# Up projection of a gated MLP: ten of 22 pairs of weight tiles from seven block products each, x normalised before the product, gated tiles split at the end

## The chip, the cores and the metric

One core of a Trainium2 chip runs the whole program. The time is the device time of one execution in microseconds (us). The engines are TensorE (PE, with its weight loads as PEld), VectorE (DVE), ScalarE (ACT), GpSimd (POOL) and SyncE (SP), whose queue starts the loads of weights. Each engine runs its own instructions in the order of the program; one that waits holds up all behind it on that engine. The program has 1 batch, 512 tokens, a model width of 1024 and fp32 data.

## The reference, cut to what matters

The layer mixes tokens in three ways, attends to a memory of 256 tokens, and ends with a gated MLP, which the change touches:

```python
x = x + memory_cross_attention(rmsnorm(x, norm_xq), rmsnorm(mem, norm_mem), ...)
x = x + conv_ffn(rmsnorm(x, norm_ffn), w_up, ffn_conv, ffn_conv_b, w_down)

def rmsnorm(x, g):                       # y = x * rsqrt(mean(x*x) + EPS), then y * g
def conv_ffn(h, w_up, conv_w, conv_b, w_down):
    u = causal_dwconv(h @ w_up, conv_w) + conv_b      # 3 taps along the tokens
    a, b = jnp.split(u, 2, axis=-1)                   # 2816 channels each
    return (jax.nn.silu(a) * b) @ w_down
```

## The kernel before, in words

Channels lie on the 128 partitions and the 512 tokens on the free axis. The model width is 8 tiles of channels, the hidden width 22 tiles for `a` and 22 for `b`. Products are made from split operands: a value is rounded to the matmul's type (`hi`, a copy on ACT) and the rest kept beside it (`lo`, a subtraction on DVE), and each product is the sum of hi by hi, hi by lo and lo by hi (`mm3`, L181-189).

The up projection (L947-959) goes over 22 pairs. Pair m makes tiles m and m+22. Each tile takes one unit of weights, 128 partitions by 1024 (8 blocks of 128 columns, one per tile of the model width): `load_unit` loads 512 KB through SP's queue into one of three buffers, `split_unit` makes hi (L164, ACT) and lo (L165, DVE) with two buffers each, and `mm3` issues 24 matmuls of 512 columns into a PSUM bank (16 by hi, L185 and L186, then 8 by lo, L188). The inputs `xf` are x times the gain, split, not yet normalised. The factor 1/rms of a token, `r_f`, comes from a column sum of squares and is multiplied in on DVE as each tile leaves PSUM (L951). Then the convolution: bias and last tap on ACT (L953), the two other taps on DVE (L955). At the end of the pair come Silu on ACT (L957), the product of the halves on DVE (L958), and the split of that gated tile into hi (L172, ACT) and lo (L173, DVE). The down projection (L961-974) is 8 tiles `dn` of 66 matmuls each.

The order of instructions on each engine isn't written out: the library's scheduler sets it when the program is built, by a model of costs of its own and by priorities in program order, so that a change of the code may reorder the program well around it. The residual input `xr` is loaded again (L804, two loads of 1 MB) from the pool "late", in memory that an earlier stage must have left.

Of the kernel before, what the change touches and what calls it, by code (L numbers as in the profile page):

```python
# [18 lines left out]
WB = (3, 2, 2)  # L19
FYP = (5, 10, 16)  # L20
GW = 7
WARM = 9
LOADS = (0, 1, 3, 2, 4, 5, 6, 7, 8, 9, 10)
KEYS_AFTER = (2, 3, 4, 5)
# [44 lines left out]
def build(nc, tc, ctx, x_t, mem_t, w, cols_d, const_d, unit_d, out_t, dbg=None):  # L69
# [9 lines left out]
    def tiles_of(which, tag, bufs, shape=(T,)):  # L79
        def alloc(name, dt=F32, n=None):  # L80
            return pool[which].tile([P, *(shape if n is None else (n,))], dt, tag=tag, name=name, bufs=bufs)
        return alloc
# [10 lines left out]
    ztile = tiles_of("cross", "z", 18)  # L93
    nwork = tiles_of("cross", "zn", 12)
    zquad = tiles_of("cross", "zq", 4, (4, T))
    hidden = tiles_of("hidden", "hid", 2 * NF)
    ptile = tiles_of("pair", "p", FYP[2])

    def dense_ps(name):
# [123 lines left out]
    def rsqrt(ps, name, scale, n=T, work=work):  # L223

        a = work(name + "a", F32, n)
        b = work(name + "b", F32, n)
        S.activation(a, ps, AF.Ln, bias=eps, scale=scale)
        S.activation(a, a, AF.Exp, scale=-0.5)
        S.activation(b, a, AF.Square, scale=math.sqrt(scale))
        V.scalar_tensor_tensor(b, ps, EPS / scale, b, ALU.add, ALU.mult)  # L230
        V.scalar_tensor_tensor(a, b, -3.0, a, ALU.add, ALU.mult)
        return a

    def column_sums(ps, src, name, n=T, work=work):

        hi, lo = split(src, lambda name, dt: work(name, dt, n), name)
        PE.matmul(ps, ones_r, hi, start=True, stop=False)
        PE.matmul(ps, ones_r, lo, start=False, stop=True)

    def head_norm(src, name, scale, n=T, work=work, psum=misc_ps):  # L240

# [30 lines left out]
                out.append(split_scaled(tiles[k + q], hi[:, s], lo[:, s], col("norm_mem", k + q)))  # L272
        return out

    def open_pool(name, stack):
        pool[name] = stack.enter_context(tc.tile_pool(name=name, bufs=1))

    open_pool("h", ctx)
    open_pool("work", ctx)
    mixing = ExitStack()  # L280
    open_pool("attn", mixing)
    open_pool("pair", mixing)
# [511 lines left out]
        V.tensor_tensor(lo, mixed[m], hi.bitcast(F32), ALU.subtract)  # L794
        ms.append((hi, lo))
    mixing.close()
    open_pool("late", ctx)
    cross = ExitStack()
    open_pool("cross", cross)

# [133 lines left out]
        dump(f"x3{m}", x3[m])  # L934
        xf.append(s)
    ps = misc_ps("xfps")
    column_sums(ps, acc, "xf")
    r_f = cp.tile([P, T], F32, tag="rl", name="r_f")
    V.tensor_scalar(r_f, rsqrt(ps, "rf", 1.0 / D), -0.5, None, ALU.mult)


    cross.close()
    open_pool("hidden", ctx)
    hid = []
    for m in range(NF):
        ab = []
        for z in range(2):  # L947
            j = m + NF * z
            ps = project(UNITS["up"] + 2 * m + z, xf, f"up{j}")
            u = awork(f"u{j}")  # L950
            V.tensor_tensor(u, ps, r_f, ALU.mult)  # L951
            c = awork(f"uc{j}")
            S.activation(c, u, AF.Identity, bias=col("ffn_conv_b", j), scale=col("ffn_conv", 3 * j + 2))  # L953
            for s in (1, 2):
                V.scalar_tensor_tensor(c[:, s:], u[:, :T - s], col("ffn_conv", 3 * j + 2 - s), c[:, s:], ALU.mult, ALU.add)  # L955
            ab.append(c)
        S.activation(ab[0], ab[0], AF.Silu)  # L957
        V.tensor_tensor(ab[1], ab[0], ab[1], ALU.mult)  # L958
        hid.append(split(ab[1], hidden, f"hid{m}"))

    unit = None  # L961
    for m in range(KC):
        ps = dense_ps(f"dn{m}")
        k = 0
        while k < NF:
            c = m * NF + k
            if c % 8 == 0:
                unit = split_unit(UNITS["down"] + c // 8)
            n = min(8 - c % 8, NF - k)
            mm3(ps, unit, [block(c % 8 + i) for i in range(n)], hid[k:k + n], k == 0, k + n == NF)  # L970
            k += n
        o = awork(f"out{m}")
        V.tensor_tensor(o, ps, x3[m], ALU.add)
        nc.sync.dma_start(out_t[m], o)

# [117 lines left out]
```

## Time and profile before

| | |
|---|---|
| three timed runs | median 1066.13 us, 1064.26 to 1066.42 |
| profiled execution | 1064.02 us, its span 1062.3 us |
| PE busy over the span | 99% |
| DVE, ACT busy over the span | 62%, 49% |
| DMA engines, 702 to 936 us (up projection) | 30% busy |
| mean granted TensorE clock | 0.999 |

In the profile a busy PE covers matmuls that overlap, so that the length of a row on PE is longer than the time from one matmul to the next. DVE's rows overlap a little as well. What an instruction takes from its engine is therefore read from start to start of rows that follow each other without idle time; the length of a row bounds it from above. Names in rows: `up` is the PSUM tile of the up projection, `dn` of the down projection, `wo` and `mk` of two projections before it (`mk`, the memory's keys, has 256 columns). `u` and `uc` are the tile after `r_f` and after the convolution.

### The profile page before, as it was taken

What the parts mean: (1) busy time and instruction counts of PE and PEld (TensorE: products, weight loads), DVE (VectorE), ACT (ScalarE), POOL (GpSimd) and SP (SyncE); (2) the same over time, 40 slices, a digit from 0 to 9 for tenths busy, and PEclk for the clock granted to TensorE, in tenths of its full rate; (3) what the DMA queues carried; (4) which work ended last, traced back from release to release, by engine and by line L of the source; (5) the groups of instructions that cost most, each with busy time, mean ns of one, the idle gap of its engine ahead of it and who ended that gap; (6) DMA issues with size and microseconds to landing.
All of it is one profiled execution on the core that took longest, in us unless ns stands there. A gap on an engine that the chain in (4) does not pass through costs nothing.

```text
span 1062.3 us, 12687 instructions
## 1 busy us (share of the span) xinstructions
PE 1050.4 (99%) x4845; PEld 855.7 (81%) x4845; DVE 661.7 (62%) x1051; ACT 521.2 (49%) x856; POOL 28.6 (3%) x82
## 2 busy tenths in 40 slices
PE   9999999999999999999999999999999999999998
PEld 7778888778888888878888887888888888888886
DVE  6796778787555443465576758677667766742221
ACT  6376758646243644565355767554444444421110
POOL 0000000101010000000000000000000000000000
PEclk9999999999999999999999999999999999999999
DMA  6323221121221111222335322122332223323330
GB/s 231 99 80 105 73 79 45 67 80 60 67 73 40 60 60 60 89 72 97 99 107 200 129 81 99 60 81 97 99 100 91 90 97 99 100 93 106 118 119 20
DMA packets 27997, 96.33 MB, mean 91 GB/s; under 512 B 3232, under 2 KB 3488, under 8 KB 27680
## 3 DMA queue, kind: packets, MB, share of 16 engines
q1 hardware_dynamic: 27648, 95.26, 27.2%
q8 instruction: 38, 0.62, 0.2%
q10 hardware_dynamic: 288, 0.27, 0.1%
q14 instruction: 23, 0.19, 0.1%
HBM read 93.41 MB, written 2.10 MB: 90 GB/s over the span
## 4 chain that ended last, share of the span: by engine, by line
PE 96%; DVE 2%; ACT 1%; issue 1%; DMA 0%; SPq 0%; POOL 0%; ACTq 0%; DVEq 0%; POOLq 0%
PE up L185 8%; PE up L188 8%; PE up L186 8%; PE g L185 4%; PE g L186 4%; PE dn L188 4%; PE dn L185 4%; PE dn L186 4%; PE g L188 4%; PE gk L355 2%; PE f L185 1%; PE wo L185 1%; PE s L186 1%; PE s L188 1%; PE wo L188 1%; PE f L188 1%
## 5 line engine op out<-in xcount | busy, mean ns | idle before, releaser
L164 ACT ACTIVATE whi<-wraw 128x1024 fp32r<-128x1024 f32 x163 | 172.6, 1059 | 306.5 <-PE up L186 89.2
L165 DVE TENSOR_TENSOR wlo<-wraw,whi 128x1024 fp32r<-128x1024 f32 x163 | 198.6, 1218 | 105.6 <-PE dn L188 49.2
L186 PE MATMUL up<-xfl,whi 128*128 128x512 f32 x352 | 138.9, 394 | 0.0
L185 PE MATMUL up<-xfh,whi 128*128 128x512 f32 x352 | 138.7, 395 | 0.0
L188 PE MATMUL up<-xfh,wlo 128*128 128x512 f32 x352 | 89.2, 395 | 0.0
L185 PE MATMUL g<-hh,whi 128*128 128x512 f32 x192 | 77.5, 404 | 1.6 <-DVE gate L371 1.6
L186 PEld LDWEIGHTS up<-xfl,whi 128*128 128x128 f32 x352 | 66.3, 188 | 15.5
L188 PEld LDWEIGHTS up<-xfh,wlo 128*128 128x128 f32 x352 | 66.3, 188 | 15.5
L185 PEld LDWEIGHTS up<-xfh,whi 128*128 128x128 f32 x352 | 66.3, 188 | 15.5
L186 PE MATMUL g<-hl,whi 128*128 128x512 f32 x192 | 75.8, 395 | 0.0
L955 DVE SCALAR_TENSOR_TENSOR uc<-u,cols,uc 128x511 f32<-128x511 f32 (+1 forms) x88 | 65.3, 747 | 1.4
L953 ACT ACTIVATE uc<-u,cols 128x512 f32<-128x512 f32 x44 | 35.8, 816 | 44.9 <-DVE u L951 44.8
L951 DVE TENSOR_TENSOR u<-up,r_f 128x512 f32<-128x512 f32 x44 | 30.2, 688 | 40.0 <-PE up L188 40.0
L188 PE MATMUL g<-hh,wlo 128*128 128x512 f32 x192 | 51.5, 401 | 0.0
L185 PEld LDWEIGHTS g<-hh,whi 128*128 128x128 f32 x192 | 36.1, 188 | 10.9 <-DVE gate L371 1.4
L188 PEld LDWEIGHTS g<-hh,wlo 128*128 128x128 f32 x192 | 35.7, 188 | 8.3 <-issue 0.5
L186 PEld LDWEIGHTS g<-hl,whi 128*128 128x128 f32 x192 | 36.2, 188 | 7.7
L371 DVE TENSOR_TENSOR gate<-g,r_x 128x512 f32<-128x512 f32 x24 | 16.4, 688 | 30.9 <-PE g L188 30.9
L186 PE MATMUL s<-hl,whi 128*128 128x512 f32 x64 | 26.1, 407 | 0.0
L185 PE MATMUL f<-hh,whi 128*128 128x512 f32 x64 | 25.7, 402 | 0.1
L185 PE MATMUL s<-hh,whi 128*128 128x512 f32 x64 | 25.6, 401 | 0.0
L186 PE MATMUL f<-hl,whi 128*128 128x512 f32 x64 | 25.6, 399 | 0.0
(1011 smaller groups left out, 2284.1 us busy)
## 6 DMA issues: line engine op xcount, KB each, us to landing
wraw<-w SPq DMA_DIRECT2D x166, 512.0 KB, 3.3
x<-x_t SPq DMA_DIRECT2D x8, 256.0 KB, 6.7
xr<-x_t SPq DMA_DIRECT2D x2, 1024.0 KB, 6.0
out<-out SPq DMA_DIRECT2D x8, 256.0 KB, 2.0
mem_sb<-mem_t SPq DMA_DIRECT2D x4, 256.0 KB, 6.5
wraw<-w SPq DMA_DIRECT2D x2, 256.0 KB, 3.9
inv<-unit ACTq DMA_DIRECT2D x1, 256.0 KB, 3.2
const<-const SPq DMA_DIRECT2D x1, 194.0 KB, 6.0
```

Of the source, the lines that this page charges most:

```text
L164: S.activation(hi, raw, AF.Copy)
L165: V.tensor_tensor(lo, raw, hi.bitcast(F32), ALU.subtract)
L185: PE.matmul(ps, hi[:, b], xh, start=first and i == 0, stop=False)
L186: PE.matmul(ps, hi[:, b], xl, start=False, stop=False)
L188: mm = PE.matmul(ps, lo[:, b], xh, start=False, stop=last and i == len(xs) - 1)
L355: pin(PE.matmul(first[h], a[:, c:c + P], b, start=k == 0 and a is hi and b is xh, stop=k == KC - 1 and b is xl))
L371: V.tensor_tensor(dst, ps, r_x, ALU.mult)
L951: V.tensor_tensor(u, ps, r_f, ALU.mult)
L953: S.activation(c, u, AF.Identity, bias=col("ffn_conv_b", j), scale=col("ffn_conv", 3 * j + 2))
L955: V.scalar_tensor_tensor(c[:, s:], u[:, :T - s], col("ffn_conv", 3 * j + 2 - s), c[:, s:], ALU.mult, ALU.add)
```

## The change

In ten pairs (`SEVEN`: 7, 8, 9, 11, 13, 15, 16, 17, 18, 20) the two units are taken as a matrix of 2 by 2 blocks (half of the model width by one of the two tiles), the tokens as two halves of 256, and the product as seven block products by Strassen's scheme in Winograd's form, not eight. Each of the seven is 4 tiles of the model width by 3 split terms, so 12 matmuls of 256 columns. Four sums of weight blocks are made on DVE per pair (`s12`, `s34`), and these and the raw blocks that are used are split: 3 times 1024 columns and once 512, on ACT and DVE. Sums of the two halves of the input (`token_forms`) are made once, after pair 4. The seven products stand in three PSUM banks (px, py, pz), and six steps of 256 columns and one copy of 512 bring them together to `u0`, `u1`.

Pairs 0 to 3 keep the raw input and the multiplication by `r_f`. After pairs 0 and 1 x is normalised once (`up_norm`: 8 times a DVE instruction of 512, and a split); the 8 other pairs that have no seven products take that input, and their convolution reads PSUM directly. A gated tile is no longer split at the end of its pair, but after pairs 18, 19 and 20 and the last. The second tile of pair 0 and pair 1 get a place in the order behind the column sum and the steps to `r_f` (`issue_after`). The pool "late" moves to the other end of the memory, and the pool "work" is closed before "hidden" is opened.

On PE at the start of the stage (xf0, xf4 are quads of the input's tiles 0 to 3 and 4 to 7, l for lo) this stood before:

```order
L186 MATMUL up0_5916<-xfl4_5830,whi101_5919 128x512
L185 MATMUL up22_5953<-xfh0_5739,whi102_5956 128x512
L186 MATMUL up22_5953<-xfl0_5740,whi102_5956 128x512
...
L186 MATMUL up22_5953<-xfl4_5830,whi102_5956 128x512
L185 MATMUL up0_5916<-xfh4_5829,whi101_5919 128x512
L185 MATMUL up22_5953<-xfh4_5829,whi102_5956 128x512
L186 MATMUL up0_5916<-xfl4_5830,whi101_5919 128x512
```

and now:

```order
L198 MATMUL up0_5917<-xfl4_5830,whi101_5920 128x512
L197 MATMUL up0_5917<-xfh4_5829,whi101_5920 128x512
L198 MATMUL up0_5917<-xfl4_5830,whi101_5920 128x512
L200 MATMUL up0_5917<-xfh0_5739,wlo101_5921 128x512 x4
L200 MATMUL up0_5917<-xfh4_5829,wlo101_5921 128x512
L249 MATMUL xfps_5896<-xfh_5897,ones_r_78 128x512
L200 MATMUL up0_5917<-xfh4_5829,wlo101_5921 128x512 x3
L250 MATMUL xfps_5896<-xfl_5898,ones_r_78 128x512
L197 MATMUL up22_5948<-xfh0_5739,whi102_5951 128x512
```

The 12 matmuls of up22 that stood between those of up0 on the first and the last tiles of the input have gone behind the column sum (xfps).

On DVE, one pair before (pair 6) has ten instructions; these are its last six:

```order
L951 TENSOR_TENSOR u28_6464<-up28_6433,r_f_5903 128x512
L165 TENSOR_TENSOR wlo116_6517<-wraw116_6514,whi116_6516 128x1024
L955 SCALAR_TENSOR_TENSOR uc28_6466<-u28_6464,cols_73,uc28_6466 128x511
L955 SCALAR_TENSOR_TENSOR uc28_6466<-u28_6464,cols_73,uc28_6466 128x510
L958 TENSOR_TENSOR uc28_6466<-uc6_6429,uc28_6466 128x512
L173 TENSOR_TENSOR hid6l_6473<-uc28_6466,hid6h_6472 128x512
```

and now, where pairs of seven products follow each other, the work of three pairs (here 15, 16 and 17) is interleaved:

```order
L1024 TENSOR_TENSOR wlo135_7685<-wraw135_7680,whi135_7684 128x1024
L1043 TENSOR_TENSOR s34_17_7689<-wraw135_7680,s12_17_7688 128x512
L1075 SCALAR_TENSOR_TENSOR uc15_7534<-u15_7526,cols_73,uc15_7534 128x511
L1075 SCALAR_TENSOR_TENSOR uc37_7538<-u37_7527,cols_73,uc37_7538 128x511
L1060 TENSOR_TENSOR w16_7660<-pz16_7573,v16_7598 128x256
L1075 SCALAR_TENSOR_TENSOR uc15_7534<-u15_7526,cols_73,uc15_7534 128x510
L1024 TENSOR_TENSOR sl12_17_7693<-s12_17_7688,sh12_17_7692 128x1024
L1075 SCALAR_TENSOR_TENSOR uc37_7538<-u37_7527,cols_73,uc37_7538 128x510
L1061 TENSOR_TENSOR w16_7660<-py16_7572,w16_7660 128x256
L1024 TENSOR_TENSOR wlo136_7697<-wraw136_7682,whi136_7696 128x512
```

The sums that empty PSUM (w16) stand between the splits of the next pair's weights (wlo, sl12) and the convolution of the pair before (uc15, uc37).

The core of the diff:

```diff
--- before.py
+++ after.py
@@ -19,6 +19,13 @@
 WB = (3, 2, 2)
 FYP = (5, 10, 16)
 GW = 7
+UB = 8
+SPARE = 2
+RAW_UP = 4
+FORMS = 4
+NORMS = {0: 2, 1: 6}
+SEVEN = (7, 8, 9, 11, 13, 15, 16, 17, 18, 20)
+SPLITS = {18: 4, 19: 14, 20: 3}
...
+    nquad = tiles_of("hidden", "nx", 4, (4, T))
+    uwork = tiles_of("hidden", "u", UB)
+    wsum = tiles_of("hidden", "ws", 2, (1024,))
+    wsumh = tiles_of("hidden", "wsh", 2, (1024,))
+    wsuml = tiles_of("hidden", "wsl", 2, (1024,))
...
-    def open_pool(name, stack):
-        pool[name] = stack.enter_context(tc.tile_pool(name=name, bufs=1))
+    def open_pool(name, stack, **kw):
+        pool[name] = stack.enter_context(tc.tile_pool(name=name, bufs=1, **kw))
 
...
-    open_pool("work", ctx)
+    small = ExitStack()
+    open_pool("work", small)
     mixing = ExitStack()
     open_pool("attn", mixing)
     open_pool("pair", mixing)
...
-    open_pool("late", ctx)
+    open_pool("late", ctx, side="right")
...
-    column_sums(ps, acc, "xf")
+    root_mm = column_sums(ps, acc, "xf")
     r_f = cp.tile([P, T], F32, tag="rl", name="r_f")
-    V.tensor_scalar(r_f, rsqrt(ps, "rf", 1.0 / D), -0.5, None, ALU.mult)
+    ra, rb = work("rfa"), work("rfb")
+    S.activation(ra, ps, AF.Ln, bias=eps, scale=1.0 / D)
+    S.activation(ra, ra, AF.Exp, scale=-0.5)
+    root_sq = S.activation(rb, ra, AF.Square, scale=math.sqrt(1.0 / D))
+    V.scalar_tensor_tensor(rb, ps, EPS * D, rb, ALU.add, ALU.mult)
+    root = V.scalar_tensor_tensor(ra, rb, -3.0, ra, ALU.add, ALU.mult)
+    V.tensor_scalar(r_f, ra, -0.5, None, ALU.mult)
 
 
     cross.close()
+    small.close()
     open_pool("hidden", ctx)
+    L, R = slice(0, T // 2), slice(T // 2, T)
     hid = []
-    for m in range(NF):
+    xn, values, halves = [], [], []
+    def up_norm():
+        k = len(xn)
+        if k % 4 == 0:
+            halves.append((nquad(f"xnh{k}", F32R), nquad(f"xnl{k}", F32R)))
+        hi, lo = (t[:, k % 4] for t in halves[-1])
+        t = hidden(f"xn{k}")
+        V.scalar_tensor_tensor(t, x3[k], col("norm_ffn", k), r_f, ALU.mult, ALU.mult)
+        S.activation(hi, t, AF.Copy)
+        V.tensor_tensor(lo, t, hi.bitcast(F32), ALU.subtract)
+        xn.append((hi, lo))
+        values.append(t)
+    def token_forms():
+        pairs = []
+        for name in ("14", "23"):
+            pairs.append([hquad(f"t{name}{z}", F32R).rearrange("p a b -> p (a b)").rearrange("p (f k n) -> p f k n", f=2, k=4)
+                          for z in "hl"])
+        for k in range(4):
+            e, o = values[k], values[k + 4]
+            f = uwork(f"tf{k}")
+            def two(t):
+                return t.rearrange("p (f n) -> p f n", f=2)
+            V.tensor_tensor(e[:, L], e[:, R], e[:, L], ALU.subtract)
+            V.tensor_tensor(two(f), two(e), o[:, None, R].to_broadcast([P, 2, T // 2]), ALU.add)
+            V.tensor_tensor(e[:, R], f[:, L], o[:, L], ALU.subtract)
+            for t, (hi, lo) in zip((e, f), pairs):
+                S.activation(hi[:, :, k], two(t), AF.Copy)
+                V.tensor_tensor(lo[:, :, k], two(t), hi[:, :, k].bitcast(F32), ALU.subtract)
+        (h14, l14), (h23, l23) = pairs
+        return {1: (h14[:, 0], l14[:, 0]), 4: (h14[:, 1], l14[:, 1]), 2: (h23[:, 0], l23[:, 0]), 3: (h23[:, 1], l23[:, 1])}
+    def half_product(ps, unit, x, behind=None):
+        (wh, wl), (xh, xl) = unit, x
+        with ExitStack() as order:
+            if behind is not None:
+                order.enter_context(tc.issue_after(behind.ins))
+            new = behind is None
+            first = PE.matmul(ps, wh[:, block(0)], xh[:, 0], start=new, stop=False, skip_group_check=not new)
+            for i in range(4):
+                if i:
+                    PE.matmul(ps, wh[:, block(i)], xh[:, i], start=False, stop=False, skip_group_check=not new)
+                PE.matmul(ps, wh[:, block(i)], xl[:, i], start=False, stop=False, skip_group_check=not new)
+            for i in range(4):
+                PE.matmul(ps, wl[:, block(i)], xh[:, i], start=False, stop=i == 3, skip_group_check=not new)
+        return first
+    def split_blocks(src, hi, lo):
+        S.activation(hi, src, AF.Copy)
+        V.tensor_tensor(lo, src, hi.bitcast(F32), ALU.subtract)
+        return hi, lo
+    def seven_products(m):
+        u = UNITS["up"] + 2 * m
+        a1, a2 = load_unit(u), load_unit(u + 1)
+        a = [(t[:, :T], t[:, T:]) for t in (a1, a2)]
+        (a11, a12), (a21, a22) = a
+        h1, l1 = wp.tile([P, 1024], F32R, tag="whi", name=f"whi{u}", bufs=WB[1]), wp.tile([P, 1024], F32R, tag="wlo", name=f"wlo{u}", bufs=WB[2])
+        split_blocks(a1, h1, l1)
+        s12, s34 = wsum(f"s12_{m}"), wsum(f"s34_{m}")
+        V.tensor_tensor(s12[:, :T], a21, a22, ALU.subtract)
+        V.tensor_tensor(s12[:, T:], a11, s12[:, :T], ALU.subtract)
+        h12, l12 = split_blocks(s12, wsumh(f"sh12_{m}", F32R), wsuml(f"sl12_{m}", F32R))
+        h2, l2 = wp.tile([P, 1024], F32R, tag="whi", name=f"whi{u + 1}", bufs=WB[1]), wp.tile([P, 1024], F32R, tag="wlo", name=f"wlo{u + 1}", bufs=WB[2])
+        split_blocks(a22, h2[:, :T], l2[:, :T])
+        V.tensor_tensor(s34[:, :T], a21, a11, ALU.subtract)
+        V.tensor_tensor(s34[:, T:], a12, s12[:, T:], ALU.subtract)
+        h34, l34 = split_blocks(s34, wsumh(f"sh34_{m}", F32R), wsuml(f"sl34_{m}", F32R))
+        (b1h, b1l), (b2h, b2l) = halves
+        px = dense_ps(f"px{m}")
+        py = misc_ps(f"py{m}")
+        pz = gdn_ps(f"pz{m}")
+        first = half_product(px[:, L], (h1[:, :T], l1[:, :T]), (b1h[:, :, L], b1l[:, :, L]))
+        half_product(px[:, R], (h12[:, :T], l12[:, :T]), t_forms[1], first)
+        v = uwork(f"v{m}")
+        S.activation(v, px, AF.Copy)
+        first_y = half_product(py[:, L], (h2[:, :T], l2[:, :T]), t_forms[4])
+        half_product(pz[:, L], (h12[:, T:], l12[:, T:]), t_forms[2])
+        half_product(px[:, L], (h1[:, T:], l1[:, T:]), (b2h[:, :, L], b2l[:, :, L]), first)
+        half_product(py[:, R], (h34[:, :T], l34[:, :T]), t_forms[3], first_y)
+        half_product(px[:, R], (h34[:, T:], l34[:, T:]), (b2h[:, :, R], b2l[:, :, R]), first)
+        w = uwork(f"w{m}")
+        u0, u1 = uwork(f"u{m}"), uwork(f"u{m + NF}")
+        V.tensor_tensor(w[:, L], pz[:, L], v[:, L], ALU.add)
+        V.tensor_tensor(w[:, R], py[:, R], w[:, L], ALU.add)
+        S.activation(u0[:, L], px[:, L], AF.Copy)
+        V.tensor_tensor(u1[:, R], w[:, R], v[:, R], ALU.add)
+        V.scalar_tensor_tensor(u1[:, L], py[:, L], -1.0, w[:, R], ALU.mult, ALU.add)
+        V.tensor_tensor(u0[:, R], px[:, R], w[:, L], ALU.add)
+        return u0, u1
+    def gated(m, us):
         ab = []
-        for z in range(2):
+        for z, u in enumerate(us):
             j = m + NF * z
-            ps = project(UNITS["up"] + 2 * m + z, xf, f"up{j}")
-            u = awork(f"u{j}")
-            V.tensor_tensor(u, ps, r_f, ALU.mult)
-            c = awork(f"uc{j}")
+            c = uwork(f"uc{j}")
             S.activation(c, u, AF.Identity, bias=col("ffn_conv_b", j), scale=col("ffn_conv", 3 * j + 2))
             for s in (1, 2):
                 V.scalar_tensor_tensor(c[:, s:], u[:, :T - s], col("ffn_conv", 3 * j + 2 - s), c[:, s:], ALU.mult, ALU.add)
             ab.append(c)
         S.activation(ab[0], ab[0], AF.Silu)
-        V.tensor_tensor(ab[1], ab[0], ab[1], ALU.mult)
-        hid.append(split(ab[1], hidden, f"hid{m}"))
+        t = hidden(f"hid{m}")
+        V.tensor_tensor(t, ab[0], ab[1], ALU.mult)
+        hid.append(t)
+    def up_product(m, z, x):
+        ps = (misc_ps if z else dense_ps)(f"up{m + NF * z}")
+        mm3(ps, split_unit(UNITS["up"] + 2 * m + z), [block(k) for k in range(KC)], x, True, True)
+        return ps
+    hs2 = []
+    def split_hidden():
+        k = len(hs2)
+        if k % 4 == 0:
+            quad[:] = [(hquad if k < 16 else nquad)(f"hh{k}", F32R)]
+        hi, lo = quad[0][:, k % 4], hidden(f"hidl{k}", F32R)
+        S.activation(hi, hid[k], AF.Copy)
+        V.tensor_tensor(lo, hid[k], hi.bitcast(F32), ALU.subtract)
+        hs2.append((hi, lo))
+    for m in range(NF):
+        if m in SEVEN:
+            us = seven_products(m)
+        else:
+            us = []
+            for z in range(2):
+                with ExitStack() as behind:
+                    for i in ([root_mm] if m == 0 and z else [root_mm, root_sq, root] if m == 1 else []):
+                        behind.enter_context(tc.issue_after(i.ins))
+                    us.append(up_product(m, z, xf if m < RAW_UP else xn))
+            if m < RAW_UP:
+                raw, us = us, []
+                for z, ps in enumerate(raw):
+                    t = uwork(f"u{m + NF * z}")
+                    V.tensor_tensor(t, ps, r_f, ALU.mult)
+                    us.append(t)
+        gated(m, us)
+        for _ in range(NORMS.get(m, 0)):
+            up_norm()
+        if m == FORMS:
+            t_forms = token_forms()
+        for _ in range(SPLITS.get(m, 0)):
+            split_hidden()
+    while len(hs2) < NF:
+        split_hidden()
 
     unit = None
     for m in range(KC):
@@ -967,9 +1130,9 @@
             if c % 8 == 0:
                 unit = split_unit(UNITS["down"] + c // 8)
             n = min(8 - c % 8, NF - k)
-            mm3(ps, unit, [block(c % 8 + i) for i in range(n)], hid[k:k + n], k == 0, k + n == NF)
+            mm3(ps, unit, [block(c % 8 + i) for i in range(n)], hs2[k:k + n], k == 0, k + n == NF)
             k += n
-        o = awork(f"out{m}")
+        o = uwork(f"out{m}")
         V.tensor_tensor(o, ps, x3[m], ALU.add)
         nc.sync.dma_start(out_t[m], o)
```

More of the change, by code (lines that the diff above doesn't have):

```diff
@@ L95, in build @@
     zquad = tiles_of("cross", "zq", 4, (4, T))
-    hidden = tiles_of("hidden", "hid", 2 * NF)
+    hidden = tiles_of("hidden", "hid", NF + SPARE)
+    nquad = tiles_of("hidden", "nx", 4, (4, T))
[3 more added lines that the diff above has]
+    wsuml = tiles_of("hidden", "wsl", 2, (1024,))
     ptile = tiles_of("pair", "p", FYP[2])
@@ L237, in column_sums @@
         PE.matmul(ps, ones_r, hi, start=True, stop=False)
-        PE.matmul(ps, ones_r, lo, start=False, stop=True)
+        return PE.matmul(ps, ones_r, lo, start=False, stop=True)
     def head_norm(src, name, scale, n=T, work=work, psum=misc_ps):
```

## The prediction, on record before the result

> **What bounds the kernel now.** I read the page's busy times and its chain by engine first, then busy time by stretch, then the chain in order of time within the up projection.
>
> ```profile
> span 1062.3 us, 12687 instructions
> PE 1050.4 (99%) x4845; PEld 855.7 (81%) x4845; DVE 661.7 (62%) x1051; ACT 521.2 (49%) x856; POOL 28.6 (3%) x82
> ...
> PE 96%; DVE 2%; ACT 1%; issue 1%; DMA 0%; SPq 0%; POOL 0%; ACTq 0%; DVEq 0%; POOLq 0%
> ```
>
> TensorE is busy for 99% of the span, and 96% of the chain that ended last is its own work. Overlapping rows exaggerate "busy", so I look at one stage. The columns below are the stretch, its length, then busy us of PE, PEld, DVE, ACT and POOL, the granted clock, DMA share and GB/s.
>
> ```profile
> core 0: us, PE busy (x) PEld busy (x) DVE busy (x) ACT busy (x) POOL busy (x), PEclk, DMA share, GB/s
> 702.00:936.00 234.00, 234.00 (x1009) 189.74 (x1008) 166.19 (x217) 103.74 (x130) 0.00 (x0) 1.00 0.30 97
> 936.00:1062.00 126.00, 122.56 (x528) 99.05 (x526) 34.38 (x34) 22.55 (x22) 0.00 (x0) 1.00 0.28 92
> ```
>
> In the up projection PE has no gap at all, at full clock; DVE is at 166.19 / 234 = 71%, ACT at 44%, DMA at 30%. So this stage gets shorter if PE gets less to do, as long as DVE can follow. The chain in order of time gives PE's pace (start, length):
>
> ```profile
> 705.34 1.86 PE up L188 x8
> ...
> 933.99 1.86 PE up L188 x8
> ```
>
> From the last eight matmuls of one tile to those of a tile 41 tiles later it is 228.65 us: 5.577 per tile of 24 matmuls, 0.2324 per matmul of 512 columns, 11.154 per pair, 245.4 for 22 pairs. PE works without a gap at this pace, so it is the bound of the stage.
>
> **The PE work removed.** A pair of seven products has 7 x 12 = 84 matmuls of 256 columns, where there were 48 of 512. The gain hangs on what a 256-column matmul with fresh weights takes. The kernel has some, in the product for the memory's keys:
>
> ```profile
> 597.81 0.28 PE L185 MATMUL mk<-memh,whi 128*128 128x256 f32 x1
> ...
> 599.46 1.11 PE L188 MATMUL mk<-memh,wlo 128*128 128x256 f32 x8
> 600.41 0.40 PE L185 MATMUL wo<-msh,whi 128*128 128x512 f32 x1
> ...
> L185 PEld LDWEIGHTS mk<-memh,whi x32: 187/188/190, 568.7 to 599.1; 128*128 128x128 f32 x32
> ```
>
> Fourteen such matmuls start from 597.81 to 599.46 (0.118 each), and eight, each on another weight block, from 599.46 to 600.41 (0.119). The weight load's own row is 188 ns, but it doesn't set the pace: those loads overlap. A pair of seven products then costs 84 x 0.118 = 9.91 us, and ten save 10 x (11.154 - 9.91) = **12.4 us** (11.6 at 0.119, and 13.9 if 256 columns cost exactly half of 512).
>
> [...]
>
> **What DVE gets instead.** DVE's prices go by start to start where rows follow each other without idle time:
>
> ```profile
> 569.43 0.42 DVE L254 TENSOR_TENSOR memq<-memq,memq 128x256 f32<-128x256 f32 x1
> 569.76 0.75 DVE L178 SCALAR_TENSOR_TENSOR xql<-xr,cols,xqh 128x512 fp32r<-128x512 f32 x1
> 570.42 0.48 DVE L178 SCALAR_TENSOR_TENSOR meml<-mem_sb,cols,memh 128x256 fp32r<-128x256 f32 x1
> ...
> 763.37 0.68 DVE L951 TENSOR_TENSOR u<-up,r_f 128x512 f32<-128x512 f32 x1
> 763.97 1.22 DVE L165 TENSOR_TENSOR wlo<-wraw,whi 128x1024 fp32r<-128x1024 f32 x1
> 765.10 1.53 DVE L955 SCALAR_TENSOR_TENSOR uc<-u,cols,uc 128x511 f32<-128x511 f32 x2
> ```
>
> That is 0.33 for 256 columns, 0.60 for 512 (0.66 with a scalar operand, I take 0.67), 1.13 for 1024. A pair of seven products has 18 instructions: three splits of 1024 (3.39), four weight sums and the split of 512 (5 x 0.60 = 3.00), five output steps of 256 (1.65), four of the convolution (2.68), the gate's product (0.60): **11.3 us, more than PE's 9.9.** A normal pair on the normalised x has 2 x 1.13 + 4 x 0.67 + 0.60 = 5.54, half of PE's 11.15. The four raw pairs keep two multiplications by r_f more (6.74). Normalising is 8 x (0.67 + 0.60) = 10.2, the sums of the input 4 x (2 x 0.33 + 3 x 0.60) = 9.8, the splits at the end 22 x 0.60 = 13.2. The sum is 27.0 + 44.3 + 113.2 + 10.2 + 9.8 + 13.2 = **217.7 us** in about 330 instructions. PE has 12 x 11.154 + 10 x 9.91 = **233.0**. So DVE still fits, but at 93%, where it had 71% by busy time. An instruction may get 15.3 / 330 = 0.046 us dearer before DVE sets the end.
>
> The row lengths bound the prices from above:
>
> ```profile
> L165 DVE TENSOR_TENSOR wlo<-wraw,whi 128x1024 fp32r<-128x1024 f32 x65 | 79.2, 1219 | 69.7 <-PE dn L188 49.2 <-ACT whi L164 15.1 <-PE up L188 5.4
> ...
> L955 DVE SCALAR_TENSOR_TENSOR uc<-u,cols,uc 128x510 f32<-128x510 f32 x44 | 32.8, 749 | 1.4
> ...
> L958 DVE TENSOR_TENSOR uc<-uc,uc 128x512 f32<-128x512 f32 x22 | 15.2, 693 | 1.1 <-ACT uc L957 0.4
> L254 DVE TENSOR_TENSOR memq<-memq,memq 128x256 f32<-128x256 f32 x7 | 3.0, 422 | 1.5 <-ACT memq L253 1.4
> ```
>
> With these a pair of seven products is 3 x 1.219 + 5 x 0.693 + 5 x 0.422 + 4 x 0.749 + 0.693 = 12.9, and the same sum over the stage comes to 246.6, above PE. [...] The trace disagrees for independent neighbours, since the 0.68 row at 763.37 has its successor 0.60 later; a rival below keeps the case.
>
> How the surplus of 1.4 us in a pair of seven products (11.3 against 9.9) is carried: before 7, 11, 13 and 20 stands a normal pair with 5.6 us to spare, and 15 to 18 follow pair 14. The order of the changed program lets DVE run ahead, as far as three raw buffers and two of each split allow: within the PE work of 15 to 18 (39.6 us) stand, by these prices, about 38 us of DVE work, the rest lies ahead of 15 and behind 18. It just fits. Short waits are to be expected there, of this kind:
>
> ```profile
> 773.91 0.69 DVE L173 TENSOR_TENSOR hid6l<-uc,hid6h 128x512 fp32r<-128x512 f32 x1 [1.33 <-ACT hid6h L172]
> ```
>
> DVE stood idle for 1.33 us for ACT's hi copy; each weight sum now has such a step (DVE sums, ACT copies, DVE subtracts, PE multiplies), and behind it in DVE's queue stand the sums that empty PSUM for the next pair. If none is passed on to PE that costs 0; if both sums of each of the four pairs 15 to 18 pass on 1.33, it costs 8 x 1.33 = 10.6. I take **3 us**, two of the eight and a little for the other pairs, where DVE has time to be ahead.
>
> **ACT.** Its lengths:
>
> ```profile
> L164 ACT ACTIVATE whi<-wraw 128x1024 fp32r<-128x1024 f32 x65 | 68.9, 1061 | 179.5 <-PE up L186 89.2 <-PE dn L186 83.9 <-issue 6.3
> ...
> L953 ACT ACTIVATE uc<-u,cols 128x512 f32<-128x512 f32 x44 | 35.8, 816 | 44.9 <-DVE u L951 44.8
> ...
> L957 ACT ACTIVATE uc<-uc 128x512 f32<-128x512 f32 x22 | 13.4, 615 | 0.0
> ```
>
> A pair of seven products has three of 1.061, two of 0.816, one Silu of 0.615, and the split of 512 and the copies v and u0, each at most as long as the Silu: 7.3 of 9.9 us. ACT fits and costs 0 by itself.
>
> **The start.** Up22 no longer fills the time in which the last tiles of the input are split:
>
> ```profile
> 689.83 0.39 PE L185 MATMUL up<-xfh,whi 128*128 128x512 f32 x1
> ...
> 692.37 0.74 DVE L178 SCALAR_TENSOR_TENSOR xfl<-xr,cols,xfh 128x512 fp32r<-128x512 f32 x1
> 693.04 0.68 DVE L816 TENSOR_TENSOR xfs<-xfs,xfs 128x512 f32<-128x512 f32 x1
> 693.64 0.75 DVE L178 SCALAR_TENSOR_TENSOR xfl<-xr,cols,xfh 128x512 fp32r<-128x512 f32 x1
> ```
>
> Up0 starts at 689.83. Its 14th matmul, on the lo part of tile 6, is due 13 x 0.2324 later, at 692.85, and that part is ready at 693.11: 0.26 us of wait. The 16th, on tile 7, is then due at 693.57 and ready at 694.39: 0.82. **+1.1 us**, between 0 (if DVE makes them earlier) and 12 x 0.2324 = 2.8, the whole of the cover taken away.
>
> **The end and the front.** The splits of the gated tiles leave the pairs and stand between and behind the last ones:
>
> ```profile
> 941.23 0.69 DVE L173 TENSOR_TENSOR hid21l<-uc,hid21h 128x512 fp32r<-128x512 f32 x1 [1.34 <-ACT hid21h L172]
> ...
> 949.41 0.39 PE L186 MATMUL dn<-hid21l,whi 128*128 128x512 f32 x1
> ```
>
> The last lo part is made at 941.92 and used at 949.41, and a down tile takes 66 x 0.2324 = 15.3 us to reach its end, so that a late split has 7.5 us of cover: 0, and a few tenths more if the cover went. In front of the stage the loads of `xr` come earlier on SP's queue and wait for an older stage to leave the memory, with later weight loads behind them:
>
> ```profile
> 516.88 0.33 SPq L156 DMA_DIRECT2D wraw<-w  x1
> 529.97 1.06 ACT L164 ACTIVATE whi<-wraw 128x1024 fp32r<-128x1024 f32 x1 [4.54 <-PE g L186]
> 554.23 0.80 SPq L804 DMA_DIRECT2D xr<-x_t  x2
> ```
>
> The weight load that now stands behind them was issued at 516.88 and first read at 529.97; with 13 us of lead I take 0, at most 2.
>
> **Sum**, against the profiled execution's 1064.02: -12.4 (PE) + 1.1 (start) + 3 (short waits) + 0 (ACT, end, front) = -8.3, so 1055.7. The three timed runs have a median of 1066.13, 2.1 above that execution; the same difference gives **1058 us**. The likeliest case's own range: all at its best, -13.9 and no wait, 1052.2; all at its worst, -11.6 + 2.8 + 2 and 5 us of waits, 1064.3.
>
> **Rivals.**
>
> *DVE's queue becomes the bound.* Its place is the runs 7 to 9 and 15 to 18. For it: 93% by start to start, and 246.6 us by lengths; the dependent steps of the convolution already follow each other by their length or more (two in 1.53 at 765.10). Against it: independent neighbours overlap, and only 71% before. It decides from 0.046 us more per instruction on. Price: 246.6 - 245.4 = 1.2, plus 1.1 at the start, plus a wait of 1.33 not covered in every second pair of seven products (5 x 1.33 = 6.7): +9.0, **1075 us**, slower.
>
> *Short waits eat the gain.* DVE fits on the whole, but all eight of those sums pass their wait on to PE: 10.6. Then -12.4 + 1.1 + 10.6 = -0.7, **1065 us**, the same. For it: the four-step way of the weight sums, and three PSUM banks per pair that DVE must empty. Against it: raw loads come early (DMA at 30%).
>
> *A fixed part per matmul.* If 256-column matmuls go at the weight load's row, 84 x 0.188 = 15.8 per pair, +46, **1112 us**. The mk rows at 0.118 are against it, and only that they are few, between matmuls of other products, leaves it a chance.
>
> **How the numbers follow.** Forecast 0.73, short waits 0.13, DVE bound 0.12, fixed part 0.02. A measurement of this kernel tells 0.2% (2.1 us) from no change: faster is below 1064.0, slower above 1068.3. Of the short-wait case some lies below 1064.0; of the forecast's upper end a little above. Faster 0.74, same 0.12, slower 0.14. The range goes from 1053.5 (a little above the best sum) to 1066.5, past the short-wait case; it leaves out the DVE bound and the fixed part, and some hundredths below.
>
> **What would show it.** Right: in pairs of seven products the matmuls follow each other at 0.116 to 0.119 us, a pair takes 9.9 to 10.2 in isolation and up to 11 within 15 to 18; PE's idle time in the stage adds up to 2 to 6 us, released by DVE; DVE is busy for 85 to 95% of the stage. Wrong: a pace above 0.13; idle of PE of more than 10 us before matmuls on `sh12`, `sl12`, `sh34` or before a product's first matmul (PSUM not emptied); DVE without a gap through 15 to 18 while PE waits; the down projection starting with waits for `hidl`.

## The result, and the profile after

The changed kernel takes 1054.76 us (median, 1054.55 to 1056.93) where the kernel before, run on the same chip beside it, takes 1065.2. The ratio is 0.9906 with a 95% interval of 0.9887 to 0.9925. The forecast was 1058 us, faster, and faster it is; the gain is 10.4 us where 8.1 was foreseen. The profiled execution took 1056.93. From the page of the changed kernel (span and busy times), then its busy time over the up projection, with the columns as before:

```profile
span 1055.3 us, 13641 instructions
PE 1041.4 (99%) x5205; PEld 866.2 (82%) x5205; DVE 711.8 (67%) x1161; ACT 552.5 (52%) x912; POOL 28.7 (3%) x82
```
```profile
693.00:928.00 235.00, 234.31 (x1418) 208.29 (x1417) 214.60 (x322) 136.97 (x191) 0.00 (x0) 1.00 0.29 97
```

DVE is busy for 214.60 of 235 us, 91%, and PE still has no gap but at the start. These are the stage's first matmul, the two matmuls that waited, and the first matmul of the down projection, in the timeline of PE:

```profile
693.08 0.39 PE L197 MATMUL up<-xfh,whi 128*128 128x512 f32 x1
...
696.42 0.50 PE L198 MATMUL up<-xfl,whi 128*128 128x512 f32 x1 [0.15 <-DVE xfl L190]
...
697.69 0.50 PE L198 MATMUL up<-xfl,whi 128*128 128x512 f32 x1 [0.53 <-DVE xfl L190]
...
928.61 0.40 PE L197 MATMUL dn<-hh,whi 128*128 128x512 f32 x1
```

By the starts, PE loses 1.22 us around the two matmuls that waited, against 0.2324 us for each. The stage takes 928.61 - 693.08 = 235.53 us, where it took 935.69 - 689.83 = 245.86. By the first matmuls of the stages, the two profiled executions differ so:

| from | before | after | difference |
|---|---|---|---|
| start to the output projection | 554.03 | 555.84 | +1.81 |
| output projection and memory's keys | 57.79 | 59.21 | +1.42 |
| cross attention to the up projection | 78.01 | 78.03 | +0.02 |
| up projection | 245.86 | 235.53 | -10.33 |
| down projection to the end of the span | 126.61 | 126.69 | +0.08 |
| outside the span | 1.72 | 1.63 | -0.09 |
| profiled execution | 1064.02 | 1056.93 | -7.09 |

Two rows lie ahead of the stage. The +1.81 comes from the first matmuls of the program, which are slow in 5 of the 14 traces of this study, this one among them and that of the kernel before not (last section). So the output projection and the up projection, where the change shows, give -8.9 us.

The +1.42 has a place. On ACT the copies of the memory's hi parts now stand in front of the hi copy of the third tile's weights, and they wait for a load, although those weights, loaded at 546.69, had landed 3.3 us later; PE waits for that hi copy (timelines of ACT, then of PE, changed kernel):

```profile
564.76 0.91 ACT L189 ACTIVATE memh<-mem_sb,cols 128x256 fp32r<-128x256 f32 x2 [5.62 <-DMA mem_sb<-mem_t]
...
567.30 1.05 ACT L176 ACTIVATE whi<-wraw 128x1024 fp32r<-128x1024 f32 x1
```
```profile
568.39 0.50 PE L197 MATMUL wo<-msh,whi 128*128 128x512 f32 x1 [1.19 <-ACT whi L176]
```

Before, two hi copies of weights stood on ACT at 561.52 and 563.62, ahead of the memory's at 564.58. On SP's queue the `xr` loads have left their place in front of the memory's load; that this is why the scheduler turned ACT's order round is argued, not tried.

### The profile page after: what moved, and what is told of

The parts are those of the page before. It is cut to its first block, busy times and chain, and to the rows that moved or that the text cites. A ratio compares the mean times of both kernels' runs of the same rounds, so it can differ in the third digit from the quotient of the medians.

```text
span 1055.3 us, 13641 instructions
## 1 busy us (share of the span) xinstructions
PE 1041.4 (99%) x5205; PEld 866.2 (82%) x5205; DVE 711.8 (67%) x1161; ACT 552.5 (52%) x912; POOL 28.7 (3%) x82
## 4 chain that ended last, share of the span: by engine, by line
PE 94%; DVE 2%; ACT 1%; issue 1%; DMA 1%; SPq 0%; POOL 0%; ACTq 0%; DVEq 0%; POOLq 0%
PE g L197 4%; PE up L200 4%; PE g L198 4%; PE up L198 4%; PE up L197 4%; PE dn L200 4%; PE dn L198 4%; PE dn L197 4%; PE g L200 4%; PE gk L368 2%; PE px L1019 2%; PE px L1017 2%; PE f L197 1%; PE s L198 1%; PE s L200 1%; PE f L200 1%
## 5 line engine op out<-in xcount | busy, mean ns | idle before, releaser
L198 PE MATMUL dn<-hidl,whi 128*128 128x512 f32 x176 | 69.3, 395 | 0.0
L197 PE MATMUL dn<-hh,whi 128*128 128x512 f32 x176 | 69.3, 394 | 0.0
L197 PE MATMUL up<-xnh,whi 128*128 128x512 f32 x128 | 50.5, 394 | 0.0
L198 PE MATMUL up<-xnl,whi 128*128 128x512 f32 x128 | 50.5, 394 | 0.0
L200 PE MATMUL dn<-hh,wlo 128*128 128x512 f32 x176 | 45.4, 395 | 0.0
L1075 DVE SCALAR_TENSOR_TENSOR uc<-u,cols,uc 128x511 f32<-128x511 f32 (+1 forms) x56 | 39.8, 749 | 0.0
L200 PEld LDWEIGHTS dn<-hh,wlo 128*128 128x128 f32 x176 | 33.2, 188 | 7.8
L198 PEld LDWEIGHTS dn<-hidl,whi 128*128 128x128 f32 x176 | 33.2, 188 | 7.7
L197 PEld LDWEIGHTS dn<-hh,whi 128*128 128x128 f32 x176 | 33.1, 188 | 7.7
L200 PE MATMUL up<-xnh,wlo 128*128 128x512 f32 x128 | 32.4, 395 | 0.0
```

The costliest lines, as they stand in the source:

```text
L197: PE.matmul(ps, hi[:, b], xh, start=first and i == 0, stop=False)
L198: PE.matmul(ps, hi[:, b], xl, start=False, stop=False)
L200: mm = PE.matmul(ps, lo[:, b], xh, start=False, stop=last and i == len(xs) - 1)
```

## The experiments

The theory: the whole gain is TensorE work that is gone, and all that was added runs beside it. Its rivals: the moved work (normalising, splits) brings a part; a matmul of 256 columns has a fixed part, or the 0.119 us contains waits; DVE is the bound, or next to it.

### The moved work alone, and eight products in place of seven

```diff
-SEVEN = (7, 8, 9, 11, 13, 15, 16, 17, 18, 20)
+SEVEN = ()                       # and no token_forms
```

> The changed kernel with an empty list of seven-product pairs: all 22 pairs are ordinary ones of 48 matmuls of 512 columns, and the sums of the input's halves are not made. Everything else of the change stays (x normalised first, gated tiles split at the end, the new order in front of the stage and at its start). Theory A (the whole gain is TensorE work that is gone): no gain is left, only the two costs that the trace of the changed kernel shows, 1.2 us of waits in the first tile and 1.4 us of a wait in the output projection before it: 1065.2 + 2.6 = 1067.8, between 1066 and 1069. Rival B (normalising and splitting elsewhere brings a part of the gain): below 1065.

Measured: 1066.58 us, ratio 1.0020 (1.0011 to 1.0029), 2.1 us slower than the kernel before. The moved work by itself brings no gain; it costs the two waits. Whether seven products would gain as much without it was not tried. In its trace the stage takes 247.08 us, which is 245.86 + 1.22, and the output projection 58.56 (+0.77: the wait there was 0.70 us, not 1.36).

```diff
-            us = seven_products(m)
+            us = [eight_products(m, z) for z in range(2)]   # 8 blocks x 3 terms x 2 halves of 256 columns
```

> As the run with only the moved work, but the ten pairs are made from eight block products: each 512-column matmul as two of 256 columns, 96 per pair, with no sums of blocks. Theory A with 0.119 us per matmul of 256 columns: 10 x (96 x 0.119 - 11.154) = 2.7 us above that run, about 1070.5. Rival C (256 columns cost exactly half of 512, and the 0.119 of the changed kernel has hidden waits on DVE in it): the same as that run within 0.5 us, about 1067.8.

Measured: 1069.3 us, ratio 1.0043 (1.0028 to 1.0058), 2.7 us above the run with the moved work alone, as theory A said. The stage takes 249.64 us there, 2.56 more, so 0.1189 us per matmul of 256 columns with none of the sums on DVE; half of 0.2324 is 0.1162. In the changed kernel it is (235.53 - 1.22 - 12 x 11.154 - 0.46 for the column sum) / 840 = 0.1190. So the 0.119 has no hidden waits in it, and a matmul of 256 columns takes 0.003 us more than half of one of 512.

### The two new waits

```diff
-        ps = (misc_ps if z else dense_ps)(f"up{m + NF * z}")
+        ps = (misc_ps if z and m else dense_ps)(f"up{m + NF * z}")
-                    for i in ([root_mm] if m == 0 and z else [root_mm, root_sq, root] if m == 1 else []):
+                    for i in ([root_mm, root_sq, root] if m == 1 else []):
```

> The changed kernel, but the second tile of pair 0 is no longer placed behind the column sum and takes its PSUM bank from the pool of the first: its first 12 matmuls stand again in front of the last ones of the first tile. Theory A: the 1.2 us of waits at the start of the stage go, 1054.8 - 1.2 = 1053.6. Rival D (r_f or the normalised x comes late by this and PE waits at pair 1 or 4 instead): 1054.8 or more.

Measured: 1056.67 us, ratio 0.9928 (0.9913 to 0.9942), in the trace 1.7 us slower than the changed kernel from the first matmul of the stage to the end: rival D. The wait at the start is gone, but the second half of the column sum went behind up22's matmuls, r_f's chain on ACT started at 703.14 (before this edit at 700.54), and a weight's hi copy stood behind it (timelines of ACT, then PE):

```profile
703.14 0.69 ACT L953 ACTIVATE rfa<-xfps,cols 128x512 f32<-128x512 f32 x1 [5.88 <-PE xfps L250]
...
705.06 1.99 ACT L176 ACTIVATE whi<-wraw 128x1024 fp32r<-128x1024 f32 x2
```
```profile
706.15 0.51 PE L197 MATMUL up<-xfh,whi 128*128 128x512 f32 x1 [1.67 <-ACT whi L176]
```

PE loses 1.9 us there and 1.0 more in pairs 8 and 9, by the kind of wait that the last run of this section shows. A place behind the column sum thus buys an early r_f with 1.2 us of idle PE.

The other wait:

```diff
+            early = [project(UNITS["wout"] + i, ms, f"wo{i}") for i in range(3)]
+            with tc.issue_after(last_hi[0].ins):      # the hi copy of the third weight unit
+                xs_mem, e_mem, r_mem = memory_prep()
```

> The changed kernel, with the hi copy of the third weight unit of the output projection placed on ACT in front of the memory's hi copies, which wait for a load; nothing of the up projection is touched. Theory A: the 1.4 us wait in front of that tile's first matmul goes, 1054.8 - 1.4 = 1053.4. Rival E (the wait moves to the memory's keys, whose product comes next): 1054.8 within 0.4 us.

Measured: 1054.92 us, ratio 0.9909 (0.9892 to 0.9925), so no difference in the total that can be told. In the trace the wait is gone and has not moved, as theory A had it: the output projection and keys take 57.71 us (57.79 in the kernel before; 59.21 in the changed kernel, 57.9 to 58.7 in seven other traces with its front). Its four runs, 1053.62, 1054.27, 1055.56 and 1055.65, against 1054.55, 1054.73, 1054.79 and 1056.93: the lowest and the highest are about 1 us down, the medians alike. The mechanism is shown, its size (0 to 1.4 us, mostly 0.6 to 0.8) only by the traces.

Then both, with the first 12 matmuls of up22 as cover and the other 12 behind the column sum:

```diff
+        if m == 0 and z:
+            ...                                        # k = 0 to 5 by hi: no constraint
+            with tc.issue_after(root_mm.ins):
+                ...                                    # k = 6, 7 by hi, and all by lo
```

> The kernel with the earlier hi copy in the output projection, and the first 12 matmuls of pair 0's second tile in front of the first tile's last ones; its other 12 stay behind the column sum, so that r_f is not later. In the run that moved the whole tile, r_f's three steps on ACT came 2.6 us later and PE waited 1.8 us for the hi copy behind them. Theory A (with the column sum in its place, only the cover is left): no wait of PE from the start of the stage to its end, 234.3 us from the first matmul of the stage to the first of the down projection (235.5 in the changed kernel), and 1054.8 - 1.2 - about 1.0 = 1052.6. Rival D (pair 1 waits all the same): 235 or more, 1053.8 or more.

Measured: 1054.7 us, ratio 0.9903 (0.9886 to 0.9919). The stage takes 235.92 us, not 234.3: rival D by its numbers. The start has no wait any more. But with 12 more matmuls in front of the column sum r_f is still 1.6 us later after the first matmul of the stage, pair 1 waits 0.5 for a hi copy, and 1.0 us came back in pairs 8 and 9. This is the largest of these waits (timeline of PE):

```profile
792.54 0.39 PE L1019 MATMUL px<-t14h,sh 128*128 128x256 f32 x1 [0.48 <-ACT sh L1029]
```

The product waits for the hi copy of a weight sum. DVE had that sum ready at 789.41. But ACT first took a copy out of PSUM, for which it stood idle until PE had finished pair 8 (timelines of DVE, then ACT):

```profile
788.73 0.68 DVE L1044 TENSOR_TENSOR s<-wraw,s 128x512 f32<-128x512 f32 x1
```
```profile
791.16 0.38 ACT L1068 ACTIVATE u<-px 128x256 f32<-128x256 f32 x1 [1.76 <-PE px L1025]
791.44 1.05 ACT L1029 ACTIVATE sh<-s 128x1024 fp32r<-128x1024 f32 x1
```

In the changed kernel ACT has the two in the other order, and PE doesn't wait:

```profile
792.61 1.05 ACT L1023 ACTIVATE sh<-s 128x1024 fp32r<-128x1024 f32 x1
793.98 0.39 ACT L1062 ACTIVATE u<-px 128x256 f32<-128x256 f32 x1 [0.33 <-PE px L1019]
```

By the trace, then, these waits come from the order that the scheduler gave to ACT, not from DVE being late. In pair 8 it is the same, with the sum ready 2.7 us before its copy. No run put ACT's order back alone.

### How much room DVE has

A weight sum made twice or four times, in each of the ten pairs:

```diff
+        for _ in range(2):                             # pad1; range(4): pad3
-        V.tensor_tensor(s34[:, :T], a21, a11, ALU.subtract)
+            V.tensor_tensor(s34[:, :T], a21, a11, ALU.subtract)
```

> The changed kernel with more work for DVE: in each of the ten pairs one weight sum of 512 columns is made twice, the second time over the first (the same values). That is 10 x 0.60 = 6.0 us more for DVE, 223.7 of 233 us by the prediction's prices. Theory A (DVE still has room everywhere, since the changed kernel's trace shows no wait of PE in these pairs): 1054.8 within 1. Rival F (in the run of pairs 15 to 18 DVE has 38 of 39.6 us already, so that most of what is added there reaches PE): 4 x 0.60 - 1.6 = 0.8 at least, and up to 2.4 if nothing can be made ahead, 1055.6 to 1057.2.

> The same with that sum made four times: 10 x 3 x 0.60 = 18.0 us more for DVE, 235.7 us by start to start, past PE's 233. If DVE's instructions cost what they take from start to start, it becomes the bound only in the runs: 15 to 18 have 38 + 7.2 = 45.2 against 39.6 (+5.6), 7 to 9 have 27.4 + 5.4 = 32.8 against 29.7 (+3.1), so 1054.8 + 8.7 = 1063.5, 1058 to 1067. If they cost their row lengths (246.6 + 10 x 3 x 0.69 = 267 against 235): 1086 or so.

Measured: 1058.51 us (ratio 0.9942, 0.9926 to 0.9959) and 1064.76 us (0.9999, 0.9990 to 1.0009). From the first matmul of the stage to the end of the span the traces have 364.6 and 371.6 us, where the changed kernel has 362.2: +2.4 and +9.4. The first has the size of rival F at its upper end, by the medians (+3.8) past it, but not its reason. Of the waits 1.5 us stand at two hi copies of weight sums, one in pairs 7 to 9 and one in 15 to 18. There too ACT had taken a copy out of PSUM first, and the sums lay ready 1.1 and 1.3 us before their copies. So this run doesn't show that DVE's room ends at 6 us more. The second is near the 8.7 foreseen, and there DVE is the bound: it is busy for 40.00 of 40 us from 860 to 900. With 18 us more, the whole gain of the change is gone.

> The changed kernel with 17 pairs from seven block products (5 to 21, no ordinary pair between them), same normalising and splits. PE: 5 x 11.154 + 17 x 10.0 = 225.8 us. DVE by start to start: 217.7 + 7 x (11.32 - 5.54) = 258.2; by row lengths 246.6 + 7 x (12.92 - 6.13) = 294. DVE must become the bound; which price it has then shows in the stage: 258 us and somewhat more (1078 to 1088) by the first, 294 and more (over 1112) by the second. If PE still set the end it would be 1054.8 - 8.1 = 1046.7.

```diff
-SEVEN = (7, 8, 9, 11, 13, 15, 16, 17, 18, 20)
+SEVEN = tuple(range(5, 22))
```

Measured: 1078.7 us, ratio 1.0130 (1.0109 to 1.0150). This run decides between the two prices of DVE's instructions. The same matmul of every second pair, in the timeline of PE, and the busy time between the first and the last of them:

```profile
848.75 0.39 PE L1013 MATMUL px<-t14h,sh 128*128 128x256 f32 x1 [0.48 <-ACT sh L1023]
...
871.40 0.39 PE L1013 MATMUL px<-t14h,sh 128*128 128x256 f32 x1 [0.48 <-ACT sh L1023]
...
916.70 0.39 PE L1013 MATMUL px<-t14h,sh 128*128 128x256 f32 x1 [0.48 <-ACT sh L1023]
```
```profile
848.70:916.70 68.00, 64.12 (x505) 61.06 (x505) 68.00 (x110) 39.94 (x54) 0.00 (x0) 1.00 0.29 94
```

DVE has no gap in 68 us, and a pair takes 67.95 / 6 = 11.325 us. The prediction's sum by start to start was 11.32, by row lengths 12.9. From the first matmul of the stage to the end of the span it takes 385.8 us; less 126.6 for the down projection that is 259.2, where the sum by start to start had 258.2. So a full DVE queue does not charge each instruction its full row here: by row lengths this stage was to take 294 us.

```diff
-SEVEN = (7, 8, 9, 11, 13, 15, 16, 17, 18, 20)
+SEVEN = (6, 7, 8, 9, 11, 13, 15, 16, 17, 18, 20)      # on top of the earlier hi copy
```

> The kernel with the earlier hi copy in the output projection and an eleventh pair of seven products, pair 6 (so 6 to 9 follow each other). Theory A: PE has 11.154 - 10.0 = 1.15 us less, and DVE 5.8 more (223.5 of 231.8): about 1053.7. Rival F (a run of four behind the sums of the input's halves leaves DVE no room): PE waits there for 2 us or more, 1056 and above.

Measured: 1056.05 us, ratio 0.9920 (0.9905 to 0.9935): rival F. PE waits 3.1 us within pairs 6 to 9, more than the 1.15 that the eleventh pair saves, and DVE has no gap there:

```profile
765.00:800.00 35.00, 33.56 (x264) 32.32 (x265) 35.00 (x57) 19.94 (x27) 0.00 (x0) 1.00 0.30 95
```

### A sum on GpSimd

```diff
-        V.tensor_tensor(s34[:, :T], a21, a11, ALU.subtract)
+        G.tensor_tensor(s34[:, :T], a21, a11, ALU.subtract)
```

> The changed kernel, with one of the four weight sums of each pair of seven products (the difference of a21 and a11) on GpSimd, which has nothing to do in this stage. DVE gets 0.60 us less per pair, 6 in all. Theory A (DVE is near its limit, but PE doesn't wait for it in the changed kernel): no change, 1054.8 within 1. Rival G (GpSimd takes several us per sum and the sum comes late, or DVE's own rows get longer beside it): PE waits at the products with the sums of a21 - a11 in 15 to 18, 1057 or more.

> The run with eleven pairs of seven products, with the same sum on GpSimd: DVE needs 10.7 us per such pair, not 11.3. Theory A (the 3 us of waits in pairs 6 to 9 come from DVE's 11.3 against PE's 10.0): of the waits about (4 x 0.60 = 2.4) go, 1056.0 - 2.4 = 1053.6. Rival G: as slow as without it or slower, 1056 or more.

Measured: 1055.81 us (ratio 0.9909, 0.9893 to 0.9924) and 1059.0 us (0.9938, 0.9921 to 0.9955), the second 3 us slower than eleven pairs without GpSimd. With ten pairs it is theory A at the edge of its range: from the first matmul of the stage to the end the trace has 362.35 us, the changed kernel 362.20. With eleven it is rival G. The first row below is the group of those sums on GpSimd, the second DVE's own first weight sum beside it (shortest, median and longest in ns); the third is the latter in the changed kernel, without GpSimd:

```profile
L1042 POOL TENSOR_TENSOR s<-wraw,wraw 128x512 f32<-128x512 f32 x10 | 17.0, 1704 | 427.4 <-DVE t23l L1001 307.1 <-DMA wraw<-w 91.1 <-DVE sl L1024 29.1
...
L1037 DVE TENSOR_TENSOR s<-wraw x10: 691/912/1662, 762.8 to 895.3; 128x512 f32<-128x512 f32 x10
```
```profile
L1037 DVE TENSOR_TENSOR s<-wraw x10: 681/684/696, 764.9 to 897.0; 128x512 f32<-128x512 f32 x10
```

GpSimd needs 1.70 us on average (1.29 to 3.53) for what DVE does in 0.60 from start to start, and DVE's sum of two tensors beside it grows from 0.68 to as much as 1.66 us. So DVE gets nothing back: with ten pairs it is busy for 217.51 of 235 us, where it was busy for 214.60 while it made these sums itself. With eleven pairs, 2.0 of the 2.9 us for which PE stands idle behind 740 us end with a lo part from DVE.

### The same ten pairs in other places

```diff
-SEVEN = (7, 8, 9, 11, 13, 15, 16, 17, 18, 20)
+SEVEN = (7, 8, 10, 11, 13, 14, 16, 17, 18, 20)        # on top of the cover at the start
```

> The run with the cover at the start restored and the earlier hi copy, where 1.0 us of the 1.2 came back as waits of PE at the first run of pairs of seven products (7 to 9), and 0.5 at pair 1. Here the ten pairs stand as 7, 8, 10, 11, 13, 14, 16, 17, 18, 20: two after each other and an ordinary pair behind, which DVE catches up in (2 x 11.3 + 5.5 = 28.1 us against PE's 31.2). Theory A (the waits come from DVE falling behind within a run): none there, the stage 234.9 us instead of 235.9, and 1053.7 if the start of the program goes alike. Rival H (DVE is behind for a reason before pair 7, the sums of the input's halves or normalising): the waits at the first pairs stay, 235.9 or more.

Measured: 1053.5 us (all runs 1053.49 to 1053.59), ratio 0.9892 (0.9875 to 0.9908). The stage takes 235.12 us, 0.8 less than with the list before; of the 1.0 us of waits in pairs 7 to 9, 0.28 are left, and there are none behind. That is theory A's number for most of it, but not its reason. The wait that went is the one of pair 9, which now is an ordinary pair and has no copy of a weight sum behind ACT's copy out of PSUM; the 0.28 at pair 8, with ACT in the same order, stand as they did. And with the list before, the longer run 15 to 18 had no wait at all: PE is busy there for 50.00 of the 50 us from 845 to 895. This is the fastest kernel of the study. Its runs all lie below those of the changed kernel, by 1.3 us of median, though the intervals of the two ratios overlap.

## Why the prediction was right, and where it was not

**What bounds the kernel, and PE's saving.** Right. The stage was PE's before and is after, and the run without block products has none of the gain. The term was 12.4 us at 0.118 per matmul; measured are 10.33 + 1.22 = 11.55, at 0.119. The prediction had that figure beside the other, from the eight matmuls of the memory's keys that follow each other without others between, and chose the fourteen that are mixed. The purer row was the better price, but by little: single steps in those rows go from 0.112 to 0.123.

**The start.** +1.1 foreseen, 1.22 found, at the two matmuls named.

**The short waits.** This step failed: 3 us were taken, from DVE's idle time for ACT in the kernel before and the run of pairs 15 to 18. The trace has none in the ten pairs: PE loses 1.2 us in the stage, all at its start, where 2 to 6 were to show the forecast right. The sum of DVE's work was right to a hundredth per pair (11.325 against 11.32), and so was the balance (93% foreseen, 91% busy). What was mis-sized is the step from there to PE: two of eight weight sums were to pass a wait on, and none did. In small variants of the kernel such waits did come, 1.0 us with the cover at the start restored and 1.5 with one weight sum doubled, at the hi copies of weight sums as the prediction had it. But DVE had those sums ready in time, and what held the copies was a copy out of PSUM that stood in front of them on ACT. DVE itself was late with four times one sum, with eleven pairs and with 17, where it had no gap in 40, 35 and 68 us.

**ACT and the end.** Both at nothing, as foreseen for the stage: the down projection to the end takes 126.69 us, before 126.61. ACT was priced by its load alone. Its order made the wait of the front, below, and those of the variants.

**The front.** 0 taken, at most 2 allowed; 1.42 found in the profiled execution; in seven others with the same front the wait is 0.55 to 0.78 six times, and once absent. The reason given, weight loads late behind `xr` on SP's queue, is not what happened. The loads came in time (the third tile's weights 17 us before their hi copy); what moved was ACT's order, where copies that wait for the memory's load now stand before a weight's hi copy. The prediction followed the queue on which the change moved something, and not the queue of the engine that waits for those loads next.

**The sum.** -11.55 + 1.22 + 1.42 = -8.9 against -8.3: waits overstated by 3, the front left out at 1.4 and PE's saving overstated by 0.9 nearly cancel, which is luck. The medians have -10.4. With that wait at 0.7 us, as in most traces, the stages give -9.6; the rest fits how many executions of each kernel had the slower first microseconds (last section). So do the 2.1 us that the forecast added for the median of three timed runs, two of which were near 1066 and one near 1064.

**The rivals.** The DVE bound is real, but lies beyond this kernel: with 18 us more on DVE the gain is gone, with seven more pairs of this kind the kernel is 1.3% slower than the one before. The price per instruction by which it would have decided here, the row's length, is excluded (with 17 pairs the stage took 259.2 us, where row lengths gave 294). A matmul of 256 columns does cost more than half of one of 512, but by 0.003 us, some 1/25 of what that rival needed.

## What to carry to other kernels

When an algorithm trades matmuls for elementwise work on a second engine, price that work by start to start of neighbouring rows, and add it up against the matmuls stretch by stretch: here 11.3 us of DVE work against 10 of PE in each new pair. What fits on the whole may fail where such pairs follow each other closely: with an eleventh pair DVE had no gap in 35 us and PE waited 3.1. And after a change that lets a scheduler reorder the program, read also the queues of engines that the change doesn't mention. The one wait that was not foreseen stood 125 us ahead of the up projection, and the waits of the small variants stood at sums that were ready: on both occasions ACT waited for something else first (5.62 us for the memory's load, 1.76 us for PE's pair 8 in the run with the cover).

## What the hardware showed that was not expected

**Two speeds of the first matmuls.** The kernel before has runs near 1064.2 and near 1066.1, and several of the others have such pairs too. The traces show a difference of that size: the first eight matmuls after the warm-up take 0.43 to 0.47 us each in some executions, 0.23 to 0.27 in others (in one trace 0.37 for the first four). The first fence is from the kernel before, the second from the changed kernel's profiled execution (timelines of PE):

```profile
6.11 1.24 PE L355 MATMUL gk<-hh,ghi 128*128 128x512 f32 x4 [0.54 <-ACT hh L347]
7.19 1.09 PE L355 MATMUL gk<-hh,glo 128*128 128x512 f32 x4
8.12 1.08 PE L355 MATMUL gk<-hl,ghi 128*128 128x512 f32 x4
```
```profile
6.21 2.07 PE L368 MATMUL gk<-hh,ghi 128*128 128x512 f32 x4 [0.64 <-ACT hh L360]
8.09 1.91 PE L368 MATMUL gk<-hh,glo 128*128 128x512 f32 x4
```

From 6.21 to 8.09 are four matmuls. The column of the granted clock has 1.00 for these stretches in both, so it doesn't show this. In 5 of 14 traces the first matmuls were slow, and in those the output projection starts at 555.8 to 556.3 us, in the nine others at 554.0 to 554.6, whatever the kernel. That the two groups of times are these is likely, but each kernel has one trace only. Why the first matmuls have two speeds isn't shown: no run here varied the warm-up. For a comparison of 1 us, times of stages from the trace are therefore better than medians of four runs.

**GpSimd beside DVE.** DVE's first weight sum got up to 0.98 us longer while GpSimd made one. One sum on GpSimd, for example, runs from 878.67 to 879.96, and DVE's, started at 878.85, takes 1.66 us, where the longest without GpSimd took 0.70. What makes DVE slower there no run shows.
